# Hybrid encoder block on one core: transform-table low parts on VectorE, later copies in the recurrence, moved sine steps, a scatter in f32r parts, and the first pair's down product ahead of the second gate

## The chip, the cores and the metric

The kernel runs on one core of one Trainium2 chip. The metric is the device time of one execution in microseconds (us), the median of repeated runs. The five compute engines of the core are TensorE (PE in the profile; PEld is its weight load), VectorE (DVE), ScalarE (ACT), GpSimd (POOL) and SyncE (SP), which only issues transfers. All transfers share 16 DMA engines.

## The reference, cut to what matters

One layer on x of 512 x 1024, everything in float32:

```python
h = rmsnorm(x, g_mix);  proj = h @ w_in            # columns: RG-LRU x, gelu gate, Hyena v/x1/x2, gates A/B
xa = dwconv(a_x, width 4)
h_a = rg_lru(xa, forward) + rg_lru(xa, reverse);   y_a = (h_a * gelu(a_gate)) @ w_a_out
filt = sin-MLP(33 -> 64 -> 64 -> 4*1024) * decay   # implicit long filters, 512 taps, two directions
z = v;  for n, gate in ((0, x1), (1, x2)): z = gate * fftconv(z, k[n], bias[n])
y_b = z @ w_b_out
x = x + (sigmoid(g_a) * y_a + sigmoid(g_b) * y_b) @ w_o
h = rmsnorm(x, g_ffn);  aff = softmax(h @ w_router)          # 16 experts
vals, idx = top_k(aff.T, 64)                                 # every expert takes 64 tokens
ye = (silu(h[idx] @ w_gate[e]) * (h[idx] @ w_up[e])) @ w_down[e]
x = x.at[idx].add(ye * vals);  return rmsnorm(x, g_final)
```

The expert weights are 16 x 3 x 8.39 MB = 402.7 MB and are read once.

## The kernel before

**The mixer half.** All matrix products of the mixer use operands split in a high part (fp32r) and a low part (the fp32 rest): three fp32r products, high x high, low x high, high x low, 24 matmuls of 128x512 per block of 128 output columns (`proj`, line 244). A weight block is loaded by SP into one of four places of `wring` (`w_raw`), its high part copied by ScalarE and its low part subtracted by GpSimd into one of two places of `whl` (`w_prep`). `slot` is the unit of order: `ahead` prepares weights up to two blocks in front, then `df.tick` runs what was put off with `df.at(lag, ...)`, then the block's matmuls follow. All engines take their work in program order.

At the start four tiles of x are loaded and scaled row by row (`square`, `rstd_of`, `norm_x`, lines 365 to 391). The filter MLP's first sine (`feat1`, `sin_of`, lines 294 to 310) is a generator: one step scales the matmul's result, four steps reduce the range on VectorE, the last is ScalarE's Sin. Before, `next(feats)` is called five times (line 373) ahead of the squares, so that all five VectorE steps stand ahead of the row scales. `hT_and_proj` transposes x, splits it, and does the first projection. Then come weight splits, the sum of the filter weights (`filt_sum`), their high parts (`filt_high`), the table KC, the second projection with the second sine in its middle (`v_slot(1, feat2)`), and only then `filt_low`, whose result `wst` is an operand of the first filter matmuls (`filt_a`, lines 462 to 465).

After the filters the long convolution goes through transform tables FC, FS (forward, line 570) and IC, IS (inverse, line 611), each in a high and a low part. `table` (line 427) makes them; by default GpSimd subtracts the low part (`e=G`), for IC VectorE does. The parts of IS are made by `is_split` inside the first round of the loop over `cjobs`, low parts on VectorE. `fwd_slot` also runs three steps of `decay_rates`, a chain of small VectorE operations. In a round, `fwd` multiplies the spectra: VectorE makes `pr`, GpSimd `y`, ScalarE the high part `yh`, VectorE the low part `yl`; `inv` reads `yh`, `yl`.

In the recurrence, `z2_load(i)` fetches the Hyena result back in eight pieces and puts off its split (`post`: one copy on ScalarE, one subtraction on VectorE) by `1 + i // 3` ticks. `lru_gates` puts eight activations on ScalarE one tick later.

**The expert half.** The experts are worked in eight pairs, one of a pair in each half of the array's columns: `rows_mm` for gate and up (line 1306), `down_part` (transposes on line 1328, matmuls on line 1341), `gather` of the 64 + 64 rows by a one-hot product (line 1272), `scatter` by the transposed one-hot scaled with the affinity (line 1356, one fp32 matmul per 128 x 512). The weights come in 192 tiles of 2.1 MB. `e_load` issues them on SP in the order of `wq` into slots: 11 fresh ones, of which 9 are used again as soon as TensorE has read their last tile. `wq` has, before, gate v, down v-1, up v for each v; the order of TensorE's work is the same. Tile 11 and 12 (`split`) are loaded in halves. `sgy` is first a slot for one weight tile, then holds silu(gate) * up (`sg`), the transposed pieces (`sts`) and the down result (`ye`). The first pair's rows are gathered between the steps of its gate product; the second pair's in one piece (line 1272, x64) between the first up product and the second gate product.

At the end the rows that the last pair touches are computed apart (`last_rows`), scaled and written by an indirect transfer.

## Time and profile before

| | us |
|---|---|
| median of 3 runs | 1637.26 (1636.01 to 1637.36) |
| the profiled execution | 1636.09 |
| its span, first to last instruction | 1634.3 |
| PE busy | 1544.8 (95%) |
| DVE / ACT / POOL busy | 590.2 / 371.8 / 376.7 |
| mean granted PE clock | 0.973 of full |
| moved by DMA | 492 MB, mean 301 GB/s |

The page cuts the span into 40 slices of 40.9 us: each digit is the busy share of a slice in tenths. Idle time of an engine costs only where the engine is what the rest waits for, so each stage has to be read by itself.

### The profile page before, as it was taken

The page shows a single profiled execution, that of the slowest core. Times are in us where ns is not written, and L with a number is a line of the kernel's source. Part 1 is how long each engine was busy: PE and PEld are TensorE (multiplying, and loading weights), DVE is VectorE, ACT ScalarE, POOL GpSimd, SP SyncE. Part 2 cuts the span into 40 slices and gives each one's busy share as a digit, 9 for nine tenths or more (in the row PEclk, how much of TensorE's full clock was granted, in tenths as well). Part 3 has the DMA queues.
Part 4 walks back from the last instruction along what each step waited for, and adds up shares of the span by engine and source line. Part 5 has one row for each costly group of instructions (what it writes and reads, how often), then busy time and mean ns, then how long its engine had stood idle before and what let it go on. Part 6 is the DMA issues. An engine that isn't in the chain of part 4 may idle for free.

```text
span 1634.3 us, 17982 instructions
## 1 busy us (share of the span) xinstructions
PE 1544.8 (95%) x7364; PEld 899.3 (55%) x7364; DVE 590.2 (36%) x879; ACT 371.8 (23%) x579; POOL 376.7 (23%) x259
## 2 busy tenths in 40 slices
PE   7999799999999999899999999999999999989997
PEld 5788799987888889733443343342343342333432
DVE  5888788866776654321001101101002002011102
ACT  5444233337655533301010000100100100100002
POOL 3556476655566642000000000000000000000000
PEclk9999899999999999999999999999999999999999
DMA  7458433443333237879999999999999999999996
GB/s 214 130 177 263 126 107 100 132 151 91 107 94 97 85 96 245 353 294 393 404 427 427 425 429 426 427 427 426 426 427 427 426 428 427 425 428 427 426 425 280
DMA packets 140833, 492.26 MB, mean 301 GB/s; under 512 B 8705, under 2 KB 103233, under 8 KB 115664
## 3 DMA queue, kind: packets, MB, share of 16 engines
q1 hardware_dynamic: 138624, 487.86, 76.1%
q0 software_dynamic: 944, 3.19, 0.6%
q8 instruction: 58, 0.95, 0.2%
q10 hardware_dynamic: 1184, 0.07, 0.0%
q14 instruction: 23, 0.19, 0.0%
HBM read 473.82 MB, written 17.30 MB: 301 GB/s over the span
## 4 chain that ended last, share of the span: by engine, by line
PE 46%; DMA 15%; DVE 2%; issue 1%; ACT 1%; POOLq 0%; SPq 0%; ACTq 0%; DVEq 0%
PE q L1306 22%; PE q L1341 10%; DMA we<-in_w_up_dram 6%; PE q L1356 3%; PE ps L244 3%; DMA we<-in_w_down_dram 3%; PE ps L1162 2%; DMA hz<-in_w_up_dram 2%; PE q L1272 2%; DMA whl<-in_w_down_dram 2%; DMA hz<-in_w_down_dram 2%; PE q L1328 1%; PE q L1399 1%; DMA out_dram<-hh 0%; DVE pm L1222 0%
## 5 line engine op out<-in xcount | busy, mean ns | idle before, releaser
L1306 PE MATMUL q<-we,xe 128*64 128x512 f32 x1088 | 342.0, 599 | 18.2 <-DMA we<-in_w_up_dram 8.5
L244 PE MATMUL ps<-hT,whl 128*128 128x512 f32 x1320 | 308.8, 392 | 4.7 <-ACT whl L129 4.1
L244 PEld LDWEIGHTS ps<-hT,whl 128*128 128x128 f32 x1320 | 247.5, 189 | 57.7 <-ACT whl L129 4.5
L1510 POOL DMA_INDIRECT out_dram<-we,idx x1 | 1.1, 1116 | 924.4 <-DVE we L135 924.4
L132 POOL TENSOR_TENSOR whl<-wring,whl 128x1024 fp32r<-128x1024 f32 x72 | 178.5, 2487 | 135.4 <-PE ps L244 59.0
L1306 PEld LDWEIGHTS q<-we,xe 128*64 128x64 f32 x1088 | 103.6, 137 | 185.7 <-issue 167.5
L1341 PE MATMUL q<-we,sgy 128*64 128x512 f32 x576 | 181.3, 619 | 4.7 <-ACT sgy L129 3.6
L132 DVE TENSOR_TENSOR xe<-q,cv 128x512 f32<-128x512 f32 (+1 forms) x22 | 11.4, 543 | 467.5 <-PE q L1306 425.7
L1306 PE MATMUL q<-hz,xe 128*64 128x512 f32 x480 | 161.5, 607 | 3.6 <-DMA hz<-in_w_up_dram 2.7
L129 ACT ACTIVATE sgy<-q 128x512 f32<-128x512 f32 x80 | 45.2, 596 | 393.0 <-PE q L1328 219.2
L132 DVE TENSOR_TENSOR xm<-xm,q 128x512 f32<-128x512 f32 x56 | 38.5, 688 | 209.3 <-PE q L1356 209.3
L1306 PE MATMUL q<-wring,xe 128*64 128x512 f32 x240 | 110.8, 611 | 0.8 <-DVE xe L132 0.8
L129 ACT ACTIVATE pm<-q 128x512 f32<-128x512 f32 x7 | 4.2, 597 | 455.3 <-PE q L1291 404.0
L1341 PEld LDWEIGHTS q<-we,sgy 128*64 128x64 f32 x576 | 54.7, 141 | 83.0 <-issue 74.5
L1306 PE MATMUL q<-whl,xe 128*64 128x512 f32 x208 | 95.0, 605 | 2.5 <-issue 2.0
L129 ACT ACTIVATE whl<-wring 128x1024 fp32r<-128x1024 f32 x72 | 76.2, 1058 | 70.0 <-PE ps L244 46.8
L244 PE MATMUL ps<-hA,whl 128*128 128x512 f32 x384 | 89.2, 392 | 0.0
L1306 PEld LDWEIGHTS q<-hz,xe 128*64 128x64 f32 x480 | 48.1, 139 | 66.2 <-issue 59.9
L244 PEld LDWEIGHTS ps<-hA,whl 128*128 128x128 f32 x384 | 72.1, 188 | 15.8
L1341 PE MATMUL q<-hz,sgy 128*64 128x512 f32 x224 | 75.5, 613 | 1.5 <-ACT sgy L129 1.5
L1356 PE MATMUL q<-sgy,pm 128*128 128x512 f32 x112 | 62.7, 642 | 0.0
L132 POOL TENSOR_TENSOR y<-pr 128x256 f32<-128x256 f32 x64 | 54.3, 872 | 34.0 <-DVE pr L132 26.9
(320 smaller groups left out, 2084.9 us busy)
## 6 DMA issues: line engine op xcount, KB each, us to landing
we<-in_w_down_dram SPq DMA_DIRECT2D x36, 2048.0 KB, 30.7
we<-in_w_up_dram SPq DMA_DIRECT2D x35, 2048.0 KB, 28.3
we<-in_w_gate_dram SPq DMA_DIRECT2D x33, 2048.0 KB, 29.8
wring<-in_w_in_dram SPq DMA_DIRECT2D x56, 512.0 KB, 4.7
hz<-in_w_gate_dram SPq DMA_DIRECT2D x14, 2048.0 KB, 27.4
hz<-in_w_down_dram SPq DMA_DIRECT2D x12, 2048.0 KB, 31.8
hz<-in_w_up_dram SPq DMA_DIRECT2D x12, 2048.0 KB, 29.5
whl<-in_w_gate_dram SPq DMA_DIRECT2D x8, 2048.0 KB, 30.8
```

Source lines behind the costliest of these rows:

```text
L129: P.activation(out=out, in_=in_, func=func, **kw)
L132: e.tensor_tensor(out=out, in0=a, in1=b, op=op)
L244: T.matmul(p, lhsT=a[:, k, :], rhs=b[k], start=(n == 0), stop=(n == 23))
L1162: T.matmul(p, lhsT=a[k][:, i * 128:(i + 1) * 128], rhs=wo[q][b][:, k, :], start=(n == 0), stop=(n == 23))
L1272: T.matmul(p[:, k * 128:(k + 1) * 128], lhsT=src[:, i, u * 128 * R + r:(u + 1) * 128 * R:R], rhs=pm[:, i, :], start=(i == 0), stop=(i == 3))
L1306: T.matmul(out[q][o:o + 64], lhsT=xe[:, k, o:o + 64], rhs=w[:, r * 2048 + q * 512:r * 2048 + (q + 1) * 512], start=(k == 0), stop=(k == KT ...
L1328: T.transpose(p[:, j * 128:(j + 1) * 128], sg[:, u * 128 * RD + i:(u + 1) * 128 * RD:RD], ident)
L1341: T.matmul(acc[hf][o:o + 64], lhsT=st[:, j % 4 * 128 + o:j % 4 * 128 + o + 64], rhs=w[:, i * 1024 + hf * 512:i * 1024 + (hf + 1) * 512], s ...
L1356: T.matmul(p, lhsT=sc[:, i * 128:(i + 1) * 128], rhs=ye[:, hf * 512:(hf + 1) * 512], start=True, stop=True)
L1399: T.matmul(p, lhsT=pm[:, i, :], rhs=xm[:, i, hf * 512:(hf + 1) * 512], start=(i == 0), stop=(i == 3))
L1510: G.indirect_dma_start(out=out, out_offset=bass.IndirectOffsetOnAxis(ap=last["idx"], axis=0), in_=yo, in_offset=None, bounds_check=S - 1, ...
```

## The change

- **Start.** `zw` is loaded on ScalarE's queue ahead of `fpar`, no longer on GpSimd's. One sine step stands ahead of the squares; four follow the fifth low part of x inside `hT_and_proj`. There all products with x's low parts come last, and `w_raw`, `w_prep` of the second block stand ahead of the sine's last step. `filt_low` moves ahead of the second projection, the table KC behind it.
- **Tables.** The low parts of FC and FS go to VectorE. The parts of IS are made ahead of the loop, low parts on GpSimd. The first `fwd_slot` runs no step of `decay_rates`.
- **Recurrence.** The split of z2 is put off by `2 + i // 2` ticks.
- **Experts.** The first pair's down product comes ahead of the second gate product, in `wq` as well; the second gather is spread over that down product. The first gather's steps move to the middle of each gate step. Three pairs of tiles are loaded in halves, the first also in quarters. `sgy` gets a pool of its own and is replaced by `sg`, `st`, `ys` when the first silu runs. One-hots are made by one operation per pair. The scatter multiplies an exact one-hot with high and low fp32r parts of the weighted down result. The last scatter of pair 5 is finished ahead of the down product of pair 6. `norms` is called a second time after the first down product.
- **End.** The last four squares of the w_o stage go to VectorE. The final product with g is made ahead of the row scale, which VectorE and ScalarE then apply to one half each.

```diff
+    zw = load(P, "zw", [33, S + 64], "zT")
+    zT, w1 = zw[:, 0:S], zw[:, S:S + 64]
     fpar = load(P, "fpar", [128, 4], "fpar")
-    zw = load(G, "zw", [33, S + 64], "zT")
-    zT, w1 = zw[:, 0:S], zw[:, S:S + 64]
...
-    for _ in range(5):
-        next(feats)
+    next(feats)
     square(0)
...
             stt(hTl[k], ps[k], cvs("g_mix", k), f(hTh[k]), ALU.mult, ALU.subtract)
+            if k == 4:
+                for _ in range(4):
+                    next(feats)
             mm.append((h, hTh, k))
             if k >= 3:
-                mm += [(l, hTh, k - 3), (h, hTl, k - 3)]
+                mm.append((l, hTh, k - 3))
+        w_raw()
+        w_prep()
         s1.append(list(feats)[-1])
-        mm += [(l, hTh, k) for k in range(KT - 3, KT)] + [(h, hTl, k) for k in range(KT - 3, KT)]
+        mm += [(l, hTh, k) for k in range(KT - 3, KT)] + [(h, hTl, k) for k in range(KT)]
...
-    w_raw()
-    w_prep()
     ws = filt_sum(*wfb[0])
+    parts = filt_high(ws)
+    filt_low(ws, parts)
     ahead()
-    parts = filt_high(ws)
+    v_slot(1, feat2)
     KCS = [table("KC", [128, 4, 256], KC_raw)]
-    v_slot(1, feat2)
-    filt_low(ws, parts)
...
-    FC = table("FC", [128, 2, 512], tabs[0])
+    FC = table("FC", [128, 2, 512], tabs[0], V)
     job_turn(0, 0)
-    FS = table("FS", [128, 2, 512], tabs[1])
+    FS = table("FS", [128, 2, 512], tabs[1], V)
...
-    def is_split():
-        for a in range(2):
-            h, l = (v[:, 2 * a:2 * a + 2].rearrange("p a b -> p (a b)") for v in IS)
-            act(h, half[a])
-            tt(V, l, half[a], f(h), ALU.subtract)
+    for a in range(2):
+        h, l = (v[:, 2 * a:2 * a + 2].rearrange("p a b -> p (a b)") for v in IS)
+        act(h, half[a])
+        tt(G, l, half[a], f(h), ALU.subtract)
...
-        for _ in range(3):
+        for _ in range(3 if (n, j) > (0, 0) else 0):
             next(rates, None)
...
-        if q == 0:
-            is_split()
...
-        df.at(1 + i // 3, post, 2)
+        df.at(2 + i // 2, post, 2)
...
-        if v == 7:
+        if v in (1, 7):
             order[:2] = order[1::-1]
...
-    split = (22 // R, wq.index(("w_up", 14, NU - 1)))
+    split = (22 // R, 22 // R + 2, 22 // R + 4, wq.index(("w_up", 14, NU - 1)))
...
+                    cuts = [0] + [1024] * (i == split[0] + 1) + [2048, 4096]
+                    for c0, c1 in zip(cuts, cuts[1:]):
                         for v_i, s_i in (wlast[-1], (v, src)):
-                            SY.dma_start(out=v_i[:, c], in_=s_i[:, c])
+                            SY.dma_start(out=v_i[:, c0:c1], in_=s_i[:, c0:c1])
...
+        pm = onehot(pr)
+        if not normed:
+            tt(V, pm, pm, win(rs2, [[1, 4], [0, 128]]), ALU.mult)
...
-        s = t_([128, S], nm="pm")
-        act(s, pa)
-        stt(s, pb, slotc, s, ALU.is_equal, ALU.mult)
-        return s
+        oh = t_([128, S], F32R, nm="pm")
+        V.tensor_scalar(oh, pb, slotc, None, op0=ALU.is_equal)
+        vl = t_([128, 1], nm="vl")
+        V.scalar_tensor_tensor(out=t_([128, S], nm="st"), in0=pa, scalar=1.0, in1=f(oh), op0=ALU.mult, op1=ALU.mult,
+                               accum_out=vl)
+        return oh, vl
...
+                    if q == 1:
+                        mid(k)
...
+    def scatter(sc, acc, tag="m", n=2):
+        oh, vl = sc
+        ys = t_([128, 2, 512], F32R, nm="ys")
+        def parts(hf):
+            act(ys[:, 0], acc[hf], AF.Copy, scale=vl)
+            stt(ys[:, 1], acc[hf], vl, f(ys)[:, 0], ALU.mult, ALU.subtract)
...
+                    for g in range(2):
+                        T.matmul(p, lhsT=oh[:, i * 128:(i + 1) * 128], rhs=ys[:, g], start=(g == 0), stop=(g == 1))
...
         if pr == 7:
+            for _ in pend:
+                pass
             acc = [p2("acc", 2), p2("acc", 2)]
-            down_part(6, acc, between=lambda j: next(pend, None))
-            ye_of(acc)
-            pend = scatter(smat(6))
+            down_part(6, acc)
+            pend = scatter(smat(6), acc)
+        elif pr == 1:
+            acc = [p2("acc", 2), p2("acc", 2)]
+            next(second)
+            next(second)
+            down_part(0, acc, between=lambda j: j > 4 and next(second, None))
+            norms()
+            pend = scatter(smat(0), acc)
...
-            rows_mm(pg, xe, "w_gate", pr, lambda k: k < 7 and next(first))
+            rows_mm(pg, xe, "w_gate", pr, mid=lambda k: k < 7 and next(first))
...
         if pr == 0:
-            *_, nxe = gather(1)
+            second = gather(1, 8)
+            nxe = next(second)
             norms()
...
+    for hf, c in enumerate(halves):
+        tt(V, yo[:, c], z[hf], gfin[:, c], ALU.mult)
     u = t_([128, 1], nm="ru")
     tt(V, u, sf[:, 4:5], sf[:, 5:6], ALU.add)
     r = scales(u, 1)
-    for hf, c in enumerate(halves):
-        stt(yo[:, c], z[hf], r, gfin[:, c], ALU.mult, ALU.mult)
+    V.tensor_scalar(yo[:, halves[0]], yo[:, halves[0]], r, None, op0=ALU.mult)
+    act(yo[:, halves[1]], yo[:, halves[1]], AF.Copy, scale=r)
```

## Rows read from the trace of the kernel before

**Rows 1.** The page, the span in 40 slices.
```profile
PE   7999799999999999899999999999999999989997
GB/s 214 130 177 263 126 107 100 132 151 91 107 94 97 85 96 245 353 294 393 404 427 427 425 429 426 427 427 426 426 427 427 426 428 427 425 428 427 426 425 280
```

**Rows 2.** Timeline of SP's queue: first issue of expert weights (start, us, instruction).
```profile
639.08 2.44 SPq L1084 DMA_DIRECT2D hz<-in_w_gate_dram  x2
```

**Rows 3.** Windows: us, busy time (count) of PE, PEld, DVE, ACT, POOL, clock, DMA share, GB/s.
```profile
700.00:730.00 30.00, 27.37 (x131) 11.50 (x130) 5.17 (x20) 0.00 (x0) 2.38 (x4) 1.00 0.66 245
730.00:760.00 30.00, 28.85 (x142) 11.22 (x144) 0.87 (x3) 6.64 (x8) 0.00 (x0) 1.00 0.98 382
...
780.00:800.00 20.00, 20.00 (x103) 8.20 (x104) 1.03 (x3) 0.00 (x0) 0.00 (x0) 1.00 0.93 379
800.00:1580.00 780.00, 741.45 (x3242) 281.98 (x3240) 77.92 (x173) 46.33 (x82) 0.00 (x0) 0.97 1.01 427
```

**Rows 4.** Timeline of the start, 0 to 49 us; idle time before and its releaser in brackets.
```profile
6.60 1.96 PE L319 MATMUL ps<-zT 33*64 33x512 f32 x2 [6.60 <-DMA zT<-in_zw_dram]
...
7.30 0.30 ACT L129 ACTIVATE rr<-ssq,eps 128x2 f32<-128x2 f32 x1
...
8.60 0.80 DVE L298 TENSOR_SCALAR sa<-ps,fpar 64x512 f32<-64x512 f32 x1 [7.71 <-PE ps L319]
...
12.12 0.15 DVE L350 TENSOR_SCALAR rm<-ssq 128x2 f32<-128x2 f32 x1
...
21.26 5.73 PE L417 MATMUL ps<-hT,whl 128*128 128x512 f32 x24
...
31.32 0.81 DVE L298 TENSOR_SCALAR sa<-ps,fpar 128x512 f32<-128x512 f32 x1 [6.67 <-PE ps L335]
...
34.17 2.51 DVE L301 TENSOR_SCALAR sk<-sk 128x512 f32<-128x512 f32 x1
...
48.77 5.63 PE L244 MATMUL ps<-hT,whl 128*128 128x512 f32 x24
```

**Rows 5.** Timeline of PE alone: the first filter matmul, and its like later.
```profile
44.03 0.76 PE L462 MATMUL ps<-wst,Sh 128*128 128x512 f32 x1 [4.87 <-DVE wst L132]
...
119.81 0.39 PE L462 MATMUL ps<-wst,Sh 128*128 128x512 f32 x1
...
122.52 5.65 PE L244 MATMUL ps<-hT,whl 128*128 128x512 f32 x24
```

**Rows 6.** Timeline around the first forward and inverse transform, 146 to 189 us.
```profile
155.46 6.62 DVE L132 TENSOR_TENSOR ICl<-raw,ICh 128x1024 fp32r<-128x1024 f32 x1
...
173.25 0.39 PE L611 MATMUL ps<-ICh,yh 128*128 128x256 f32 x1 [1.01 <-ACT yh L129]
...
181.48 1.28 DVE L132 TENSOR_TENSOR ISl<-xa,ISh 128x512 fp32r<-128x512 f32 x2
182.22 1.40 PE L611 MATMUL ps<-ISl,yh 128*128 128x256 f32 x4 [6.77 <-DVE ISl L132]
...
188.82 0.40 PE L570 MATMUL ps<-eoh,FCh 128*128 128x256 f32 x2
```

**Rows 7.** Timeline of the recurrence's first rounds.
```profile
359.64 11.07 PE L244 MATMUL ps<-hT,whl 128*128 128x512 f32 x48
...
374.76 12.81 PE L244 MATMUL ps<-hT,whl 128*128 128x512 f32 x48 [4.05 <-ACT whl L129]
```

**Rows 8.** Timeline of the first pair, and of the end.
```profile
710.71 3.65 PE L1306 MATMUL q<-hz,xe 128*64 128x512 f32 x16 [0.38 <-DVE xe L132]
...
774.22 8.22 PE L1272 MATMUL q<-pm,xm 128*128 128x128 f32 x64 [1.33 <-DVE pm L1262]
...
1545.89 1.12 PE L1356 MATMUL q<-sgy,pm 128*128 128x512 f32 x2
...
1616.09 7.04 PE L1341 MATMUL q<-hz,sgy 128*64 128x512 f32 x32
...
1628.00 1.41 DVE L135 SCALAR_TENSOR_TENSOR we<-q,rr,we 128x512 f32<-128x512 f32 x2
```

More of the change, by code (lines that the diff above doesn't have):

```diff
@@ L1188, in block_kernel @@
     close_("xo", "m", "bx", "A")
-    open_("T", "rout", "we1")
+    open_("T", "rout", "we1", "sgy")
     sgy = t_([128, 4 * 1024], nm="sgy")
     hh = t_([128, 4, D], nm="hh")
-    sg, ye = sgy[:, 0:2048], sgy[:, 2048:3072]
-    sts = [sgy[:, 3072 + i * 512:3584 + i * 512] for i in range(2)]
     we1 = t_([128, 8 * 1024], nm="we1")
@@ L1311, in rows_mm @@
             e_load()
+    sgt = []
     def silu(pg, g):
-        act(sg[:, g * 512:(g + 1) * 512], pg[g], AF.Silu)
+        if not sgt:
+            close_("sgy")
+            open_("sg")
+            sgt.append(t_([128, 2048], nm="sg"))
+        act(sgt[0][:, g * 512:(g + 1) * 512], pg[g], AF.Silu)
     def up_part(pr, xe):
@@ L1430, in block_kernel @@
             rows_mm(pg, xe, "w_gate", pr, lambda k: next(pend, None))
+            if pr == 1:
+                for g in range(4):
+                    silu(pg, g)
+                *_, nxe = gather(2)
+                up_part(1, xe)
+                xe = nxe
+                continue
             sc = smat(pr - 1)
+            ng = gather(pr + 1)
+            next(ng)
             acc = [p2("acc", 2), p2("acc", 2)]
@@ L1434, in block_kernel @@
             silu(pg, 3)
-            ye_of(acc)
-            pend = scatter(sc)
+            pend = scatter(sc, acc, *(("gu", 4) if pr == 6 else ()))
         if 0 < pr < 7:
-            *_, nxe = gather(pr + 1)
+            *_, nxe = ng
         up_part(pr, xe)
         if pr == 0:
-            *_, nxe = gather(1)
+            second = gather(1, 8)
+            nxe = next(second)
             norms()
@@ L1479, in z_of @@
             z.append(p2("gu", 4))
-            T.matmul(z[-1], lhsT=ident, rhs=ye[:, c], start=True, stop=False)
+            T.matmul(z[-1], lhsT=ident, rhs=hh[:, 3, c], start=True, stop=False)
     rest = all_rows()
```

77 lines of the change are left out of this document (38 added, 39 removed).

## Prediction

> **What bounds the kernel now.** Read the 40 slices first [rows 1]: TensorE is at 9 tenths nearly everywhere, but in the second half GB/s stands at 427 and does not move. A rate that is flat over 20 slices is a limit, so two stages with two limits must be kept apart. Then SP's queue [rows 2]: the 402.7 MB of expert weights are first issued at 639.1 us. At 427 GB/s they need 402.7 / 0.427 = 943 us, and from 800 to 1580 the stream runs at that rate without a gap [rows 3]. From there on TensorE's work costs nothing as long as slots come free in time. So the time is: the moment when the first weights can be issued (set by TensorE's work in the mixer, which frees the memory), plus 943 us, plus what the stream loses while it starves, plus a tail behind the last weight. The change can win in the first, third and fourth term only.
>
> The stream starves between 700 and 800: 30 us at 245, 30 at 382 and 20 at 379 GB/s [rows 3] are 12.8 + 3.2 + 2.2 = 18.2 us lost against 427. In the mixer I read the timeline for places where TensorE waits, since elsewhere it streams at its pace (24 matmuls of 128x512 in 5.65 us, 0.235 each [rows 5]). There are three large ones: 4.87 us ahead of 44.03 [rows 5], 6.77 ahead of 182.22 [rows 6], 4.05 ahead of 374.76 [rows 7]. The change aims at each of them.
>
> **Start.** Four of the sine's five VectorE steps leave the path to the row scale. They and the first stand between 8.60 and 12.12, where the scale begins [rows 4]. With only the first step ahead (it ends at 9.40) the scale begins 2.7 us earlier. If zw lands earlier on ScalarE's queue, the square root at 7.30 is the next thing late: it ends at 7.60, and the gain is at most 4.5. No row prices zw on that queue, so both ends stay; I take 3.5. ScalarE's first squares wait for x, so the extra issue on its queue is covered. The four steps (12.12 - 9.40 = 2.7 us) now stand ahead of VectorE's last three low parts of x, which the first projection needs. Eight matmuls (1.9 us) moved ahead cover most of that; a step that meets a GpSimd operation can take 2.51 us, as one does at 34.17 [rows 4]. So 0.8 to 3.3 us come back, I take 1.5. The projection ends near 25 instead of 27 (21.26 + 5.73).
>
> Behind it, `filt_low` no longer stands behind the second sine, and KC's copy and subtraction stand behind that sine on ScalarE and GpSimd, so the 2.51 us step there loses its cause. The sine's chain, which begins at 31.32 and lets the filter start at 44.03, then ends before TensorE is through its two projections: 25 + 2 x 5.65 + 1 to 2 for the sine's own matmul gives 37 to 38.5. The filter starts 5.5 to 7 us earlier and without a wait. There is a second part: from 44.03 to 48.77 the first filter group takes 4.74 us, its like from 119.81 to 122.52 takes 2.71 [rows 5]; the 2.0 us between them is the clock after the wait. Together 8, between 6 and 10. `w_raw` passes no instruction on SP's queue.
>
> **Tables.** TensorE waits for yh (until 173.25) and then for the low part of IS (until 182.22) [rows 6]. The change makes that part early, and takes the small `decay_rates` operations from between. What is late next is yh. If it comes no earlier than now, the two inverse products are 48 matmuls of half width, 45 of them from 173.25 on: 45 x 0.118 = 5.3 us, and the next forward product starts at 178.6 instead of 188.82: 10.2 us. That includes the slow clock behind the wait. GpSimd loses FC's and FS's low parts. If the products on VectorE then start earlier, up to 3 us more, about 12.5 in all. Against it: the low parts on VectorE may come late, which costs TensorE in the forward product. ICl, the same operation on the same engine, took 6.62 us, while two half tables (IS's low parts) took 1.28 together [rows 6]; the difference is GpSimd, which splits weights beside the first. So a table part costs 1.3 to 6.6 us, and which it is depends on whether GpSimd runs a weight split at that moment. I take one short, one half covered: 10, between 2 and 12.5. ScalarE now waits for the load of IS in the middle of its queue; behind it stand one weight split and one convolution copy, which TensorE needs a block later (5.65 us of cover).
>
> The Trainium skill (SBUF — State Buffer, "Who interferes with whom") speaks against this move: a VectorE operation with two SBUF inputs and a GpSimd operation that reads SBUF take an exclusive lock in turn, and the loser waits for the whole instruction. The 6.62 us row agrees. By that rule alone both new subtractions wait in full, which is the first rival below.
>
> **Recurrence.** TensorE waits 4.05 us for a weight's high part that stands on ScalarE behind eight gate activations and three z2 copies; with z2 put off, the weight ahead of it on ScalarE goes out earlier and so does everything behind. The 48 matmuls after the wait took 12.81 us, the 48 before 11.07 [rows 7]: 1.7 of clock. 5.8 at most, 4 if the clock stays; I take 5.5. The last two z2 pieces come at tick 5, their first reader at tick 6: covered by one block and the gates' matmuls. Sum for the mixer: 8 + 10 + 5.5 = 23.5 us, and everything behind moves by it.
>
> **First pairs.** The stream's last dry spot is around 790, where slots wait for TensorE. A gate step takes 5.2 us, 3.65 of it matmuls [rows 8]; with the gather in the middle of the step the wait of 0.38 and the drain go, some 0.6 x 7 = 4 us. The second gather (1.33 + 8.22 us) no longer stands whole between the up product and the next release: two of its eight steps do (2 us), plus the wait for silu * up and the first transposes (4 us), so 3 to 4 us more. But the next down step carries four gather steps (7.0 + 0.8 + 4.1 = 12 us for slots that the stream fills in 4.2 MB / 0.427 = 9.8), which returns 2. Silu now waits for the whole slot, 0.7. So 5 us of the 18.2, between 1 and 8. The finer halves free slots earlier, but the stream is held later again, so I count them at nothing.
>
> In later pairs the scatter's matmul of 1.12 us [rows 8] becomes two of 0.235. That is 5 us per pair on TensorE, hidden behind the stream. The second `norms` (four ScalarE operations in the down product), the one-hots (two whole operations for eight small ones) and the squares on VectorE lie beside other work: 0, within 0.5 each way.
>
> **Tail.** The last 32 down matmuls (7.04 us) start at 1616.09, when the last chunk lands, because TensorE is behind [rows 8]. With 10 us less scatter work in the last two pairs it can keep up to the landing of the tile before, and 2.5 us go. At the very end 1.41 us of products become one half on each engine, 0.6. Together 3, between 0.6 and 4.5.
>
> Sum: 23.5 + 5 + 3 = 31.5. The profiled execution took 1636.1 (its span 1634.3 plus 1.8), so 1604.6 in its frame; the median is 1.2 above it, so 1605.8.
>
> **The rivals.**
> 1. VectorE's table parts wait in full (place: 147 to 180 us). Two parts of 6.6 us ahead of the forward product and ICl again behind: TensorE waits some 8 us there, and the win of the tables falls from 10 to 2. 1636.1 - 23.5 + 1.2 = 1613.8. For it: the ICl row. Against: GpSimd has 5 us less to do there.
> 2. The first pair's order leaves the stream as dry as before, and TensorE stays behind at the end: 1605.8 + 5 + 2.4 = 1613.2. For it: the down product now stands directly behind the up product, with its transposes uncovered.
> 3. Slower: in each later pair the slots come free too late. Place: the weighting of the down result (ScalarE and VectorE, once per half) ahead of the scatter's matmuls, inside the gate product. TensorE is busy 741 of 780 us there [rows 3], and part of that is slow pace, so new waits beyond roughly 15 us a pair of 118 us make the stream dry; each further us costs 6. To undo 31.5 us takes 20 us a pair, and at 21 it gives 1643. Against: the half is prepared a gate step (3.65 us) ahead.
> 4. Nothing: the first issue at 639.1 is held by something that TensorE doesn't set, and 1637. Against: the issue follows the memory's release.
>
> **How the numbers follow.** Forecast 0.58 (1600 to 1612); rival 1 0.16; rival 2 0.12; better than forecast, down to 1594, 0.06; rival 4 0.03; rival 3 0.05. Predicted 1606. The range 1596 to 1620 takes the forecast, both partial rivals and the bounds of the start and the tables, and leaves out 2 in 10 or less. A measurement can tell about 0.2% (3.3 us) from no change. Faster 0.92, same 0.03, slower 0.05.
>
> **What would show it.** Expert weights first issued near 615.6 instead of 639.1; no wait above 2 us ahead of the first filter group, of the IS product and of the recurrence's second round; GB/s in the 100 us after the first gate product nearer 427; last chunk followed by 4 to 5 us of matmuls instead of 7. I am wrong if FS's low part makes TensorE wait over 3 us, if the first issue comes later than 622, or if a slice after 800 falls below 420 GB/s.

## The result, and the profile after

The changed kernel takes 1619.32 us (median of 4 runs, 1619.3 to 1619.81) against 1636.63 (4 runs, 1634.52 to 1637.36): ratio 0.9897, 95% interval 0.988 to 0.9914. The gain is 17.3 us where 31.5 were worked out; the time lies at the slow edge of the range, 0.7 us inside it. The profiled run has a span of 1617.6 us, 16.7 below that of before.

First the page of the changed kernel, the span in 40 slices, and the first issue of expert weights on SP's queue:

```profile
PE   8999999999999999899999999999999989989997
GB/s 205 191 178 240 119 118 118 118 163 85 98 112 91 86 97 319 352 320 389 386 427 426 427 427 427 427 427 427 427 427 427 426 427 427 426 427 427 426 425 282
```
```profile
623.18 2.43 SPq L1083 DMA_DIRECT2D hz<-in_w_gate_dram  x2
```

The stream stands at 427 as in [rows 1], so the sum of the prediction keeps its form. The weights are first issued at 623.18 instead of 639.08 [rows 2]: 15.9 of the 16.7 us are won in the mixer, where 23.5 were forecast, and 0.8 in the expert half, where 8 were. By terms, each read as the lead of a TensorE mark over its like of before:

```
term            forecast   measured   read from
start              8          7.7     x product after the first filter group, 41.11 against 48.77
tables            10          7.1     lead grows to 14.8 at the x product after the first inverse products
recurrence         5.5        1.1     lead 14.8 at 336.40, 15.9 at the first weight issue
first pairs        5          0.5     last 32 matmuls 16.45 earlier, less 15.9
tail               3          0.25    from those to the end 18.0 instead of 18.2
```

**Start.** Timeline of the changed kernel (start, us, engine, line, operation; in brackets the idle time before and what ended it):

```profile
7.82 0.15 DVE L352 TENSOR_SCALAR rm<-ssq 128x2 f32<-128x2 f32 x1
...
19.18 2.80 POOL L134 TENSOR_TENSOR whl<-wring,whl 128x1024 fp32r<-128x1024 f32 x1 [3.17 <-ACT whl L131]
19.78 2.48 DVE L309 TENSOR_SCALAR sa<-sa 64x512 f32<-64x512 f32 x1
...
22.98 0.50 PE L423 MATMUL ps<-hT,whl 128*128 128x512 f32 x1 [2.21 <-DVE hT L137]
...
38.41 0.39 PE L468 MATMUL ps<-wst,Sh 128*128 128x512 f32 x1
```

The row scale begins at 7.82 instead of 12.12 [rows 4], and the first filter matmul has no wait any more (4.87 in [rows 5]). But the sine's last step takes 2.48 us beside a GpSimd weight split, and behind it TensorE waits 2.21 for a low part of x and then runs slowly (granted clock 0.66 from 24.6 to 29.6 us).

**Tables.** Timeline of the first forward and inverse transform:

```profile
140.61 2.27 DVE L134 TENSOR_TENSOR FCl<-pr,FCh 128x1024 fp32r<-128x1024 f32 x1
...
144.00 1.21 DVE L134 TENSOR_TENSOR FSl<-pr,FSh 128x1024 fp32r<-128x1024 f32 x1
...
147.24 4.29 DVE L134 TENSOR_TENSOR ICl<-raw,ICh 128x1024 fp32r<-128x1024 f32 x1
...
152.32 0.63 ACT L131 ACTIVATE ISh<-xa 128x512 fp32r<-128x512 f32 x1 [7.60 <-DMA xa<-in_IS_dram]
...
154.98 0.76 ACT L131 ACTIVATE gx<-ps,cv 128x512 f32<-128x512 f32 x1
...
157.23 2.34 DVE L134 TENSOR_TENSOR pr<-ps,K 128x1024 f32<-128x1024 f32 x2
...
165.62 0.38 PE L617 MATMUL ps<-ICh,yh 128*128 128x256 f32 x1 [2.21 <-ACT yh L131]
```

The wait of 6.77 for IS [rows 6] is gone. In its place ScalarE stands 7.60 us ahead of the copy of IS, with its copy for `gx` behind it. VectorE waits 4.25 us for that copy, its first product `pr` stands behind its own part of `gx`, and TensorE then waits for `yh`.

**Recurrence.** Timeline of its first round, the kernel before, and after it the changed one:

```profile
341.63 0.75 DVE L132 TENSOR_TENSOR yt<-ps,qs 128x256 f32<-128x256 f32 x2
...
351.20 5.63 PE L244 MATMUL ps<-hT,whl 128*128 128x512 f32 x24
```
```profile
326.82 0.17 DVE L134 TENSOR_TENSOR sp<-sp,sp 128x16 f32<-128x16 f32 x1
...
328.07 0.42 DVE L134 TENSOR_TENSOR yt<-ps,qs 128x256 f32<-128x256 f32 x1
...
336.40 5.63 PE L246 MATMUL ps<-hT,whl 128*128 128x512 f32 x24
...
342.93 2.35 POOL L134 TENSOR_TENSOR whl<-wring,whl 128x1024 fp32r<-128x1024 f32 x1
342.97 3.47 DVE L134 TENSOR_TENSOR xl<-xa,xh 128x512 fp32r<-128x512 f32 x2
...
345.90 0.79 PE L880 MATMUL ps<-xl,wgh 128*128 128x512 f32 x1 [2.95 <-DVE xl L134]
...
349.88 21.93 PE L246 MATMUL ps<-hT,whl 128*128 128x512 f32 x96
```

The 4.05 ahead of the second round [rows 7] is gone, 96 matmuls run through from 349.88. A new wait of 2.95 stands one step earlier, for `xl`, which VectorE makes beside a GpSimd split. From 336.40 to 349.88 it is 13.5 us; in the kernel before the same step took 8.4 (351.20 to 359.64). Part of the difference begins earlier: the steps of `decay_rates` that the first `fwd_slot` no longer runs (from 326.82 to 328.15) now stand ahead of `yt`, which comes 8.3 us ahead of the x product instead of 9.6. GpSimd's `z` and weight splits behind it, and SP's issue of the gates' weight (335.79, before 349.34), come 1.2 to 1.3 us later against the x product as well, and VectorE waits 2.65 us for that weight instead of 0.84.

**First pairs.** SP's queue, where each issue tells that a slot came free. The kernel before, and after it the changed one, behind the first up product:

```profile
773.33 0.38 SPq L1084 DMA_DIRECT2D we<-in_w_down_dram  x1
789.48 0.33 SPq L1084 DMA_DIRECT2D whl<-in_w_down_dram  x1
...
796.35 0.80 SPq L1084 DMA_DIRECT2D we<-in_w_down_dram  x2
803.22 0.80 SPq L1084 DMA_DIRECT2D hz<-in_w_down_dram  x2
```
```profile
755.71 0.38 SPq L1083 DMA_DIRECT2D we<-in_w_gate_dram  x1
769.98 0.33 SPq L1083 DMA_DIRECT2D whl<-in_w_gate_dram  x1
...
781.20 0.80 SPq L1083 DMA_DIRECT2D we<-in_w_gate_dram  x2
792.42 1.08 SPq L1083 DMA_DIRECT2D hz<-in_w_gate_dram  x2
```

The first slot comes 14.3 us behind the last of the up product instead of 16.2, but the next two follow 11.2 us apart instead of 6.9, and the stream fills a pair of slots in 9.8. What the stream loses against 427 GB/s, added up over windows, from 45 to 140 us behind the first issue: 16.7 us before, 14.7 after. From 140 to 185 us: 2.2 before, 3.9 after.

**Tail.** TensorE's timeline of the last down product, changed kernel:

```profile
1591.90 1.93 PE L1357 MATMUL q<-we,st 128*64 128x512 f32 x6 [1.07 <-DMA we<-in_w_down_dram]
...
1599.64 7.04 PE L1357 MATMUL q<-hz,st 128*64 128x512 f32 x32
```

TensorE enters this product (its first transposes) at 1569.87, 946.7 us behind the first weight issue; before it was 1589.13, 950.05. It is 3.4 us better off (the scatter had been counted as 10 us less work), and loses 2.8 of it again to tiles that land whole: the product takes 36.8 us to 1606.7, before 34.0 (to 1623.1). Its first eight matmuls take 2.89 us instead of 1.94, with a wait of 0.77 for a tile on PEld, and the wait of 1.07 above stands at a later tile.

### The profile page after: what moved, and what is told of

The parts are those of the page before. It is cut to its first block, busy times and chain, and to the rows that moved or that the text cites. A ratio compares the mean times of both kernels' runs of the same rounds, so it can differ in the third digit from the quotient of the medians.

```text
span 1617.6 us, 17938 instructions
## 1 busy us (share of the span) xinstructions
PE 1530.1 (95%) x7364; PEld 894.3 (55%) x7364; DVE 590.4 (37%) x865; ACT 372.4 (23%) x569; POOL 372.4 (23%) x254
## 4 chain that ended last, share of the span: by engine, by line
PE 36%; DMA 26%; DVE 3%; ACT 1%; issue 0%; POOLq 0%; SPq 0%; DVEq 0%; ACTq 0%
PE q L1311 15%; PE q L1357 11%; DMA we<-in_w_up_dram 8%; DMA we<-in_w_gate_dram 4%; DMA whl<-in_w_down_dram 4%; DMA wring<-in_w_gate_dram 4%; PE ps L246 3%; PE ps L1161 2%; DMA hz<-in_w_up_dram 2%; DMA hz<-in_w_gate_dram 2%; DMA we<-in_w_down_dram 2%; PE q L1275 2%; PE q L1343 1%; PE q L1383 1%; PE q L1421 1%
## 5 line engine op out<-in xcount | busy, mean ns | idle before, releaser
L1311 PE MATMUL q<-we,xe 128*64 128x512 f32 x1088 | 362.2, 606 | 21.2 <-DMA we<-in_w_up_dram 11.0
L1311 PE MATMUL q<-hz,xe 128*64 128x512 f32 x480 | 172.3, 612 | 3.9 <-DMA hz<-in_w_up_dram 2.7
L1357 PE MATMUL q<-we,st 128*64 128x512 f32 x576 | 168.8, 617 | 3.8 <-ACT st L131 2.7
L134 DVE TENSOR_TENSOR xe<-q,cv 128x128 f32<-128x128 f32 (+1 forms) x28 | 12.4, 461 | 295.6 <-PE q L1311 235.0
L131 ACT ACTIVATE ys<-q,vl 128x512 fp32r<-128x512 f32 x14 | 9.6, 687 | 399.5 <-PE q L1383 319.8
L131 ACT ACTIVATE st<-q 128x512 f32<-128x512 f32 x32 | 19.1, 597 | 355.2 <-PE q L1343 355.2
L1357 PEld LDWEIGHTS q<-we,st 128*64 128x64 f32 x576 | 51.2, 140 | 76.1 <-issue 65.3
L137 DVE SCALAR_TENSOR_TENSOR ys<-q,vl,ys 128x512 fp32r<-128x512 f32 x14 | 10.5, 748 | 167.0 <-ACT ys L131 167.0
L1357 PE MATMUL q<-hz,st 128*64 128x512 f32 x224 | 68.5, 612 | 1.4 <-ACT st L131 1.4
L1357 PE MATMUL q<-whl,st 128*64 128x512 f32 x128 | 59.5, 611 | 3.0 <-DMA whl<-in_w_down_dram 1.6
```

What stands on the lines that cost most here:

```text
L131: P.activation(out=out, in_=in_, func=func, **kw)
L134: e.tensor_tensor(out=out, in0=a, in1=b, op=op)
L137: V.scalar_tensor_tensor(out=out, in0=a, scalar=s, in1=b, op0=op0, op1=op1)
L1311: T.matmul(out[q][o:o + 64], lhsT=xe[:, k, o:o + 64], rhs=w[:, r * 2048 + q * 512:r * 2048 + (q + 1) * 512], start=(k == 0), stop=(k == KT ...
L1357: T.matmul(acc[hf][o:o + 64], lhsT=st[:, j % 4 * 128 + o:j % 4 * 128 + o + 64], rhs=w[:, i * 1024 + hf * 512:i * 1024 + (hf + 1) * 512], s ...
```

## The experiments

The question was where 14 us of the forecast went. Each kernel is the changed one with the edit shown; each was run once, the last one five times. Four of them (the changed kernel, and the seventh, eighth and tenth below) have the same mixer, and issue the first expert weights at 623.18, 623.68, 624.77 and 623.41: differences under 1.6 us there say little, so I read stages between TensorE marks where I can.

**The low part of xa first.**

```diff
     wg_load(0)
-    wg_prep(0)
     parts_of(0)
     parts_of(1)
+    wg_prep(0)
```

> The changed kernel with one move: the two low parts of xa (xl, VectorE) are put ahead of the gates' weight split (wgh, wgl) in program order, so that they fill the 2.65 us in which VectorE waits for that weight's load and are done before GpSimd's weight split at 342.93. Theory A (the recurrence gained 1 and not 5.5 us because xl, 3.47 us for two, ran beside that GpSimd split): xl takes about 1.3 us for two, the wait of 2.95 us ahead of the matmul of xl goes, the slow matmuls behind it too; the first expert weights are issued 3.5 to 5 us earlier, at 618 to 619.7 instead of 623.18. Theory B (the wait only moves: wgl now meets the same GpSimd split, or the weight's load is as late): under 1.5 us, issue after 621.7.

1620.0 us, first weights at 623.94. Theory B: the wait moved. Timeline:

```profile
339.04 4.00 DVE L134 TENSOR_TENSOR xl<-xa,xh 128x512 fp32r<-128x512 f32 x2
...
342.96 3.06 DVE L847 CAST wgh<-wgr 128x512 fp32r<-128x512 f32 x1
...
343.37 2.35 POOL L134 TENSOR_TENSOR whl<-wring,whl 128x1024 fp32r<-128x1024 f32 x1
...
346.17 0.77 PE L880 MATMUL ps<-xh,wgh 128*128 128x512 f32 x1 [3.69 <-DVE wgh L847]
```

`xl` now meets GpSimd's product `z` (4.00 us for two), and the weight's copy `wgh`, 0.43 us in the sixth kernel, meets the split. The order on VectorE isn't the cause; GpSimd's work beside it may be.

**The z2 copies early again.**

```diff
-        df.at(2 + i // 2, post, 2)
+        df.at(1 + i // 3, post, 2)
```

> The changed kernel with one part undone: the z2 copies are due at 1 + i // 3 again as before. Theory A (putting z2 off removed the stall of the kernel before ahead of the recurrence's second round, 4.05 us and 1.7 of clock, and brought a new one of about 5 ahead of the first): the new one goes (xl for two takes about 1.3 us, no wait near 3 us on it), the old one comes back (a wait of 3.5 to 4.5 us for a weight's high part some 25 us later), and the first expert weights are issued within 1.5 us of 623.18. Theory B (the new stall has another cause and stays): old and new stall together, issue at 627.5 to 629.5.

1623.12 us, first weights at 625.45, 2.3 us later than in the changed kernel and so outside theory A's 1.5. Theory A as to the waits: `xl` is short again, and the old stall is back.

```profile
335.16 5.63 PE L246 MATMUL ps<-hT,whl 128*128 128x512 f32 x24
...
341.73 1.29 DVE L134 TENSOR_TENSOR xl<-xa,xh 128x512 fp32r<-128x512 f32 x2
...
361.23 12.78 PE L246 MATMUL ps<-hT,whl 128*128 128x512 f32 x48 [4.58 <-ACT whl L131]
```

From the x product at 335.16 (336.40 in the changed kernel) to the first weight issue it takes 290.3 us, 286.8 with the copies late. Putting z2 off is worth 3.5 us, not 5.5: it takes one stall away and brings another, because the weight's high part that had waited behind the copies now comes early, and GpSimd's split of it falls beside `xl`.

**The load of IS issued earlier.**

```diff
     tabs.append(table_load("IC", G, "raw"))
+    half = [t_([128, 512], nm="xa") for _ in range(2)]
+    for a in range(2):
+        G.dma_start(out=half[a], in_=A["IS"][:, a * 512:(a + 1) * 512])
...
-    half = [t_([128, 512], nm="xa") for _ in range(2)]
-    for a in range(2):
-        G.dma_start(out=half[a], in_=A["IS"][:, a * 512:(a + 1) * 512])
```

> The changed kernel with one move: the two loads of IS are issued on GpSimd's queue right behind those of FC, FS and IC, ahead of the FC and FS splits, instead of behind them. Theory A (the tables gained 7.1 and not 10 us because ScalarE's copy of IS waits 7.60 us for its load and the convolution copy that the products need stands behind it): that wait falls under 1 us, VectorE's idle time of 4.25 ahead of gx goes, the products begin 3 to 4 us earlier, TensorE's waits for yh (2.21 and 1.03) go and with them the slow matmuls to 174; the first expert weights are issued 3 to 5.5 us earlier, at 617.7 to 620.2. Theory B (the products are held by GpSimd's sums or by the K load): under 1 us, issue after 622.2.

1625.69 us, first weights at 626.43: worse, and neither theory. The load was issued at 144.37, 6.0 us behind the start of the second x product (6.2 in the changed kernel), after 14.76 us on GpSimd's queue with the weight splits behind it; between 140 and 160 us TensorE was busy 14.4 of 20 us (19.7 in the changed kernel). TensorE waited 5.61 us there, for the first of those splits. So the load doesn't wait for its place in the queue. What it waits for stayed open: the profile names one VectorE instruction in one run and another in the next.

**The first projection's weight split behind the sine.**

```diff
-        w_raw()
-        w_prep()
         s1.append(list(feats)[-1])
+        w_raw()
+        w_prep()
```

> The changed kernel with one move: in the first projection the split of the next weight is put behind the sine on ScalarE, so GpSimd's part of it starts some 2.5 us later and no longer meets the sine's last VectorE step. Theory A (that step took 2.48 instead of 0.42 us because of the GpSimd split of 2.80 us beside it, and TensorE's wait of 2.21 for the low part of x behind it is its price): the step takes under 0.6 us, the first projection ends near 22.5 instead of 24.66, the first filter matmul starts near 36.2 instead of 38.41, and the first expert weights are issued 1.5 to 2.5 us earlier, at 620.7 to 621.7. Theory B (the filter's start is set by the second sine or the clock, or the next weight is late then): under 0.7 us at the first filter matmul.

1619.33 us, first weights at 621.74. Theory A for the step, and a surprise for the time:

```profile
19.45 0.42 DVE L309 TENSOR_SCALAR sa<-sa 64x512 f32<-64x512 f32 x1
```

The first projection ends at 22.2, and the second x product behind the filters starts at 136.77; in the ten kernels with the changed kernel's start it is at 137.7 to 139.4. So 0.9 to 2.6 us are won, yet the time is the same. They are lost in the first down product: the first slot comes 148.4 us behind the first issue, not 146.8. Windows of 3.5 us behind TensorE's wait of 2.21 for the one-hot, this kernel, then the seventh below (busy time of PE, PEld, DVE, ACT, POOL; granted clock; DMA share; GB/s):

```profile
759.50:763.00 3.50, 2.81 (x8) 0.77 (x8) 0.00 (x0) 0.60 (x1) 0.00 (x0) 0.50 1.04 440
```
```profile
761.40:764.90 3.50, 3.50 (x18) 1.38 (x18) 0.00 (x0) 0.60 (x1) 0.00 (x0) 1.00 1.01 431
```

The same instructions behind the same wait get the lower clock level (0.50) in one run and the upper in the other. In the nine kernels with the same work up to there the first slot comes anywhere from 145.5 to 148.4 us: at 145.5 to 145.6 where the clock stays up, at 146.7 to 147.0 where it falls for the one-hot product and the first transposes, at 148.3 to 148.4 where it stays down for the eight matmuls too. (The third kernel, at 149.7, had lost 1 us more of the stream before.)

**IS split behind the convolution copy.** (The four lines move as they are.)

```diff
     cjobs = [(n, j) for n in range(2) for j in range(4)]
     ahead()
     df.tick()
+    for a in range(2):
+        h, l = (v[:, 2 * a:2 * a + 2].rearrange("p a b -> p (a b)") for v in IS)
+        act(h, half[a])
+        tt(G, l, half[a], f(h), ALU.subtract)
```

> The changed kernel with one move: the split of IS (two copies on ScalarE, two subtractions on GpSimd) is put behind one more weight split and the convolution copy gx in program order, still ahead of the first products' yh; its load stays where it is. Moving the load itself had made things worse, since it waits for its memory and not for its queue. Theory A (the tables gave 7.1 and not 10 us because gx stands on ScalarE behind copies that wait for the load): the copy of gx runs before 149 instead of at 154.98, VectorE's first product starts 2 to 5 us earlier than 157.23, the waits of 2.21 and 1.03 for yh go, and the first expert weights are issued 2 to 5 us earlier than 623.18. Theory B (the products are then held by ICl, 4.29 us beside a GpSimd split, and by GpSimd's own queue): under 1 us.

1615.53 us, first weights at 619.75. Theory A: from the second x product (138.33) to the x product behind the first inverse products (174.93) it takes 36.6 us, 40.4 in the changed kernel. `gx` is copied at 144.17, and:

```profile
145.25 1.46 POOL L134 TENSOR_TENSOR eo<-z 128x256 f32<-128x256 f32 x2
145.86 6.63 DVE L134 TENSOR_TENSOR ICl<-raw,ICh 128x1024 fp32r<-128x1024 f32 x1
146.64 4.76 POOL L134 TENSOR_TENSOR whl<-wring,whl 128x1024 fp32r<-128x1024 f32 x2
...
153.86 2.35 DVE L134 TENSOR_TENSOR pr<-ps,K 128x1024 f32<-128x1024 f32 x2
```

`pr` starts 3.4 us earlier, 2.4 against the start of the stage, although ICl (6.63 us) has become the longer. So ScalarE's wait was what the tables lacked.

**One split on VectorE, the wrong one.**

```diff
-        tt(G, l, r, f(h), ALU.subtract)
+        tt(V if i == 28 else G, l, r, f(h), ALU.subtract)
```

> The changed kernel with one instruction on another engine: the low part of the one weight that GpSimd splits at 342.93 (2.35 us) is made on VectorE, behind xl. Putting xl earlier had only made other VectorE instructions meet that split (the weight's copy took 3.06 us). Theory A (VectorE loses about 3 us to that one GpSimd instruction, whichever of its own is next to it): no VectorE instruction between 341 and 345 takes over 1.1 us beyond its pace, the wait of 2.95 us falls under 1, the slow matmuls behind it go, and the first expert weights are issued 3 to 5 us earlier, at 618.2 to 620.2. Theory B (what is late is the weight's load, or the 1.2 us more on VectorE hold the gates' steps): under 1 us.

1618.17 us. The index was one off: the split moved to 332.12, GpSimd's own stayed at 340.74, and `xl` with it at 3.43 us; the stage took 13.0 us. It only shows that moving another split leaves `xl` as it was; the right one is in the eleventh kernel.

**The gather spread over three tiles.**

```diff
-            down_part(0, acc, between=lambda j: j > 4 and next(second, None))
+            down_part(0, acc, between=lambda j: j > 4 and j % 2 and next(second, None))
```

> The changed kernel with one move: in the first pair's down product the last six steps of the second gather come one after every second row group from the fifth on, instead of after each from the fifth on, so two fall into each of three weight tiles instead of four and two. Theory A (the stream was as dry as before behind the first pair because two weight tiles of the down product are released 11.2 us apart where the stream fills one in 9.8): the releases behind the first (146.8 us after the first issue) come 9.3 to 9.9 us apart instead of 11.2, 11.2 and 6.9, GB/s from 784 to 814 is above 420 instead of 406, and the last weights land 1 to 2.6 us earlier. Theory B (the total of work up to the next gate product decides, not its spacing): within 0.5 us.

1617.04 us. Theory A: slots come 9.9, 9.9 and 9.45 us apart. Windows of the changed kernel, then of this one:

```profile
764.00:784.00 20.00, 20.00 (x104) 9.17 (x104) 1.17 (x4) 1.20 (x2) 0.00 (x0) 1.00 0.96 376
784.00:814.00 30.00, 30.00 (x142) 11.17 (x142) 5.19 (x11) 5.44 (x6) 0.00 (x0) 1.00 0.98 405
```
```profile
764.00:784.00 20.00, 20.00 (x104) 8.77 (x102) 0.88 (x3) 3.51 (x5) 0.00 (x0) 1.00 1.00 406
784.00:814.00 30.00, 30.00 (x142) 11.11 (x140) 5.48 (x12) 3.03 (x4) 0.00 (x0) 1.00 1.01 426
```

From 140 to 250 us behind the first issue the stream loses 1.6 us, against 2.5 to 3.3 in the kernels that got the same clock there without the edit (the fifth, eighth and ninth). So the spacing is worth 0.9 to 1.7 us.

**The tiles before the last in halves.**

```diff
-            elif i < len(wq) - 2:
+            elif i < len(wq) - 4:
                 SY.dma_start(out=v, in_=src)
+            elif i == len(wq) - 3:
+                for c0 in (0, 2048):
+                    for v_i, s_i in (wlast[-1], (v, src)):
+                        SY.dma_start(out=v_i[:, c0:c0 + 2048], in_=s_i[:, c0:c0 + 2048])
```

> The changed kernel with one change at the end: the pair of weight tiles before the last is loaded in halves (four DMAs instead of two). Theory A (the tail gained 0.25 and not 3 us because TensorE isn't behind there: it waits for these two tiles to land whole, at 1591.90, and has 62 matmuls and two groups of transposes, 14.8 us, left when the stream has 4.2 MB, 9.8 us, left): TensorE starts on the first halves some 4 us earlier, and from the landing of the second halves to the end of the last down matmul it takes 10 to 12.5 us instead of 14.8; the time falls by 2 to 4 us. Theory B (the last tile's own eight pieces land as late as TensorE reaches them now, or the more DMAs slow the landing): under 0.7 us.

1617.57 us, with the first weights issued 1.6 us later than in the changed kernel. The wait at that tile is gone. The last 32 matmuls start 973.1 us behind the first issue; in the fifth and ninth kernel, with the same clock in the first pair, it is 976.1 and 975.4. So 2.3 to 3 us, theory A by its size, though the time alone fell by 1.75 and not by its 2 or more. But TensorE now runs without a wait from 1576.86 to the end of the down product: it was nearly behind, and is the bound now.

**FC and FS on GpSimd again.**

```diff
-    FC = table("FC", [128, 2, 512], tabs[0], V)
+    FC = table("FC", [128, 2, 512], tabs[0])
-    FS = table("FS", [128, 2, 512], tabs[1], V)
+    FS = table("FS", [128, 2, 512], tabs[1])
```

> The changed kernel with one part undone: the low parts of FC and FS are made on GpSimd again. Measure: from the start of the second x product behind the filters (139.35 in the changed kernel) to the x product behind the first inverse products (179.78), 40.4 us there, 40.1 to 41.0 in the kernels of this study that have the same work in that stage, 47.6 before the change. Theory A (the move to VectorE is worth something, since VectorE's two parts took 2.27 and 1.21 us and no one waited for them): 41.5 to 44 us, with a wait of 0.5 to 2.5 us ahead of the forward product for FS's low part. Theory B (VectorE's parts wait in full for GpSimd and cost what they give): 40 us or less.

1617.66 us; the stage takes 40.7 us (137.70 to 178.36), between both theories, and the same as with the parts on VectorE. TensorE waits here:

```profile
144.91 0.50 PE L576 MATMUL ps<-eoh,FSl 128*128 128x256 f32 x2 [0.56 <-POOL FSl L134]
```

and gets it back. Moving the two parts is worth nothing as long as ScalarE waits for IS. The 7.1 us come from IS's early parts and from `decay_rates`' steps, which stood ahead of them on VectorE; no run separates these two.

**The first pair's order undone.** In the order of tiles and of the loop, down 0 goes back behind gate 1 and `gather(1)` whole behind up 0:

```diff
-        if v in (1, 7):
+        if v == 7:
...
-            second = gather(1, 8)
-            nxe = next(second)
+            *_, nxe = gather(1)
```

> The changed kernel with one part undone: the first pair's down product stands behind the second gate product again and the second gather stands whole behind the first up product. Measure: what the stream loses against 427 GB/s from 45 us after the first weight issue on, 17.8 to 18.9 us in the changed kernel (from 45 to 140 us 14.7, from 140 to 185 us 2.8 to 3.9 by the clock that the down product gets), 19.2 before the change (16.7 and 2.2). Theory A (the first gate product's half of the edit won 2 us and the moved down product gave 1 to 1.7 of it back): 14.3 to 15 from 45 to 140 and 2 to 3 from 140 to 185, in all 16.3 to 18, so the time is within 1.5 us of the changed kernel's 1619.3, or better. Theory B (the order is worth 3 us or more as forecast): over 20 in all.

1619.24 us, the time of the changed kernel. The stream loses 14.7 us from 45 to 140 and 3.3 from 140 to 185, in all 18.6, a little over theory A's bound and far from B's. The new order wins nothing. The 2 us between 45 and 140 stay here, so they aren't its work; they lie in the first gate product, whose gather stands in the middle of a step now, but no run undoes that edit alone.

**All moves together.** The fourth, fifth and seventh edits, the split of the weight with index 29 on VectorE, and halves for the first three tile pairs of the last down product:

```diff
-        tt(G, l, r, f(h), ALU.subtract)
+        tt(V if i == 29 else G, l, r, f(h), ALU.subtract)
...
-            elif i < len(wq) - 2:
+            elif i < len(wq) - 8:
                 SY.dma_start(out=v, in_=src)
+            elif i < len(wq) - 2:
+                for c0 in (0, 2048) if (len(wq) - i) % 2 else ():
+                    for v_i, s_i in (wlast[-1], (v, src)):
+                        SY.dma_start(out=v_i[:, c0:c0 + 2048], in_=s_i[:, c0:c0 + 2048])
```

> The changed kernel with the moves that the runs before bore out, together: the split of IS behind the convolution copy gx; the first projection's weight split behind the sine; the one weight split that GpSimd makes beside xl (at 342.93) on VectorE behind xl, which an earlier run had missed by one weight; the second gather's steps spread over three weight tiles; the first three tile pairs of the last down product loaded in halves. Expected by stages: second x product behind the filters near 136.8 instead of 138.1 to 139.4; from there to the x product behind the first inverse products 36.6 us instead of 40.4; in the recurrence from the product at 336.40 to the one at 349.88 10 to 11 us instead of 13.5 (theory A: the GpSimd split is what makes xl late; theory B: it is not, and 13 to 14.4 stay); first expert weights at 613.5 to 616.5 instead of 623.2 to 624.8; stream loss from 140 to 250 us behind that 1.5 to 2 instead of 2.8 to 3.9; the last 32 down matmuls start 1 to 2.5 us nearer to the stream's end. Time 1605 to 1610.

1608.04 us, first weights at 612.88. The recurrence settles theory A: with that one GpSimd instruction on VectorE,

```profile
336.19 1.29 DVE L134 TENSOR_TENSOR xl<-xa,xh 128x512 fp32r<-128x512 f32 x2
...
336.93 0.50 PE L880 MATMUL ps<-xl,wgh 128*128 128x512 f32 x1 [0.74 <-DVE xl L134]
...
337.40 1.22 DVE L134 TENSOR_TENSOR whl<-wring,whl 128x1024 fp32r<-128x1024 f32 x1
...
339.56 10.60 PE L246 MATMUL ps<-hT,whl 128*128 128x512 f32 x46
```

the stage takes 9.2 us (330.32 to 339.56) instead of 13.5, and 9.9 in the next kernel, which has the same edit. The tables' stage takes 37.0. The recurrence and the first weights came out better than their bounds (10 to 11 us, 613.5). One expectation failed: the stream lost 4.2 us from 140 to 250, since the wait for the one-hot again left TensorE at the lower clock.

**And the one-hot ahead of the up product.**

```diff
+        if pr == 0:
+            pm1 = onehot(1)
+            tt(V, pm1, pm1, win(rs2, [[1, 4], [0, 128]]), ALU.mult)
         up_part(pr, xe)
         if pr == 0:
-            second = gather(1, 8)
+            second = gather(1, 8, pm1)
```

(`gather` takes a one-hot that is handed to it as it is.)

> The kernel of the run before (all moves together) with one more: the second gather's one-hot and its weighting (two VectorE instructions of 0.68 us) are made ahead of the first up product instead of behind its last product with silu. Theory A (TensorE's wait of 2.21 us for that one-hot, and the half-speed matmuls that followed it in that run, 1.06 us instead of 0.59 each, are what puts the first release of the down product at 148.3 us behind the first weight issue, and at 145.5 to 149.7 in the others): the wait falls under 0.7, the first release comes at 143 to 145.5, the stream loses 0.5 to 2 us from 140 to 250 instead of 4.2, and the time is 1604 to 1606.5 against 1608.0. Theory B (the wait moves to the product with silu, behind which the transposes stand): over 147, and 1607.5 to 1609.

1605.03 us (median of 5, 1604.51 to 1606.64), ratio to the kernel before 0.981, interval 0.9797 to 0.9824. Theory A: the gather starts without a wait, the first slot comes at 143.2 us, and from 140 to 250 the stream loses nothing. TensorE's timeline, the kernel before this one, then this:

```profile
747.17 2.64 PE L1279 MATMUL q<-pm,xm 128*128 128x128 f32 x16 [2.21 <-DVE pm L134]
```
```profile
745.37 2.15 PE L1280 MATMUL q<-pm,xm 128*128 128x128 f32 x16
```

## Why the prediction was right or wrong

The form held: the first weight issue, plus a stream at 427 GB/s, plus its dry spots, plus a tail. The direction held in every term. Each size but the start's was clearly too large, for the most part for one reason: I took a stall away and priced what is late next only on the engine that had stalled. That the time still lies in the range, by 0.7 us, is luck: the range was meant to take a rival or the bounds of the start and the tables, and what filled it is rival 2's loss together with a recurrence that had no bound below 4.

**Start: right in size.** The row scale came 4.3 us earlier (3.5 taken, 4.5 the bound). The first projection ended 2.2 us earlier (24.66, before 26.82), so 2.1 of them came back through the low parts of x (1.5 taken, 3.3 the bound), and the slow clock behind the wait cost 1.6 more (14 matmuls in 4.94 us instead of 3.33), which I had not counted. What I overlooked stands in the sentence on `w_raw`: I looked only at SP's queue. The `w_prep` that goes with it has a GpSimd half that stands beside the sine's last step; with both behind the sine (fourth kernel) that step takes 0.42 us and 0.9 to 2.6 us come back.

**Tables: mis-sized, 10 against 7.1.** "If the products on VectorE then start earlier, up to 3 us more" went the other way: `pr` started 1.4 us later than the lead of the start gives (before, it began at 163.44; less 7.7 is 155.8). The failed step is the one on ScalarE's wait for the load, which I covered with a block of 5.65 us: what stands behind it, the copy for `gx`, is waited for at once by VectorE, which has its products behind it, and not only by TensorE a block later. The fifth kernel moves that one wait and wins 3.8 us, so 10.9 in all were there. VectorE's two table parts took 2.27 and 1.21 us, inside my bounds, but the move wins nothing (ninth kernel).

**Recurrence: wrong, 5.5 against 1.1.** The wait and the slow clock behind it went, as forecast. The step that failed is "the weight ahead of it on ScalarE goes out earlier and so does everything behind", which I booked as gain alone. What comes earlier also collides earlier: GpSimd's split of that weight now runs beside `xl`. By the second kernel the edit is worth 3.5 us, and by the last two the collision cost 3.5 to 4.2. The 2.4 us between 3.5 and 1.1 are there in the second kernel already: from the x product to the second round it needs 26.1 us, the kernel before 23.6. Of these 1.5 lie in the gates' step (335.16 to 345.14 is 10.0 us, 8.4 before), where the weight lands later because `decay_rates`' last steps moved ahead of `yt`: so the rows read, no run undoes that move. That is a part of the change which I had counted as gain alone, in the tables. The rest I did not pin down.

The Trainium skill states this collision (SBUF — State Buffer, "Who interferes with whom"): a VectorE instruction with two SBUF inputs, or a copy or scalar operation in a mode with two ports, and a GpSimd instruction that reads SBUF shut each other out for the whole instruction. The rows agree, also for the copy `wgh` (0.43 to 3.06 us) and the sine's step (0.42 to 2.48). I had weighed it for the tables and, by the 2.51 of [rows 4], for the start's sine steps. In the recurrence I had not, where neither of the two instructions that meet, `xl` and the split, was touched by the change.

**First pairs: wrong, 5 against 0.5.** This is rival 2, in its place and its size (7.4 us with the tail, measured 7.2), but not by its reason: the last kernel keeps the down product and its transposes directly behind the up product, and loses nothing from 140 us on. The 4 us taken for the gate step gave 2 at most. "The next down step carries four gather steps, which returns 2" stopped at one tile: the tile behind it is late as well, and a stream that fills a pair of slots in 9.8 us feels the latest of all releases, each less 9.8 us for every one ahead of it. After: 769.98, 781.20 - 9.8 = 771.4, 792.42 - 19.6 = 772.8. Before, 15.9 us earlier: 773.6, 770.6, 767.7. The latest moved by 0.8, not by the first release's 3.6.

**Tail: wrong, 3 against 0.25.** TensorE did enter the last product 3.4 us better off. But I had read it as late throughout, and 3.4 us earlier it is ahead of two tiles that land whole, and waits. In pieces the same head start gives 2.3 to 3 us (eighth kernel).

Rival 1 did not happen, rival 3 neither: from 800 us on the page's slices are at 425 to 427. By my own test (first issue later than 622) the forecast's path was wrong, which 623.18 says. The 1643 of rival 3 was added up wrongly: 1605.8 + 6 x 6 is 1641.8.

## What to carry to other kernels

When an instruction is freed to run earlier, list what will then run beside it, and above all the GpSimd and VectorE instructions that meet; the removed wait is only half of the sum. In a stream fed by slots, put every release against the fill time and take the latest, since an earlier first release alone buys nothing. And a wait on an in-order queue costs what stands behind it there, on whichever engine that is needed first.

## What the runs showed of the hardware

A VectorE instruction does not lose only to one GpSimd instruction. ICl, 1.2 us of work for 128 x 1024 (the split at 337.40 in the eleventh kernel is of that shape), took 6.63 us in the fifth kernel, from 145.86 to 152.49, while GpSimd ran four instructions in a row up to 151.40; in the changed kernel, beside three, 4.29. In both it ends 1.1 us behind the last of them.

The same code behind the same wait of 2.21 us on TensorE got the full clock in some runs and half of it in others, up to 2.9 us apart at the next slot. A wait costs this chance on top of its own length, and a change of 2 us upstream can vanish in it, as in the fourth kernel.
